# Gates as three rounded-fp32 products, two more pairs down in seven of eight products, and norm factors sent as rows through DRAM

## The chip, the core and the metric

The kernel runs on one core of a Trainium2 chip. The metric is the device time of one execution in microseconds; the time of the kernel before is the median of three runs. Five engines work side by side, each with its own queue in order: PE (matmuls), DVE, ACT and POOL (elementwise work), and SP, which here only issues DMAs. A DMA that waits for data holds back every later DMA of SP's queue.

## The reference

One step of a decoder layer for 2048 prompt tokens and 8 sampled tokens (together 2056), width D = 1024, all in fp32:

```python
xn = _rmsnorm(x, norm1_g)
z = einsum('btd,de->bte', xn, w_in)          # xr 512 | gr 512 | q 512 | k 128 | v 128
xr, gr, q, k, v = split(z, IN_SPLITS)
xc, new_conv = _causal_conv(xr, conv_buf, conv_w, conv_b)
...
r = sigmoid(_block_diag(xf, gate_a_w, gate_a_b))   # the two gates of the RG-LRU, 8 blocks of 64x64
i = sigmoid(_block_diag(xf, gate_x_w, gate_x_b))
... # h = a_t * h + u_t over the tokens
rec = hs * gelu(gr);  att = sliding-window attention(q, k, v)
mix = concatenate([_rmsnorm(rec, rec_norm_g), _rmsnorm(att, attn_norm_g)])
h = x + einsum('bte,ed->btd', mix, w_out)
hn = _rmsnorm(h, norm2_g)
ff = silu(hn @ w_gate) * (hn @ w_up)          # width 2816
y = h + ff @ w_down
...
y_prompt = _rmsnorm(yp, final_norm_g)
```

Every `_rmsnorm` needs one factor for each token, 1/sqrt(mean(x^2) + eps). The kernel keeps activations with features on the partitions and tokens along the columns, so a factor must be known on all 128 partitions, as one row repeated.

## The kernel before, in words

The work has two stages. **Stage A** (to about 610 us) goes through four token groups, `SUBS`, of 520, 512, 512 and 512 tokens. For each: normalise x, the input projection (`ip{s}_{u}`, u = 0 to 13: xr chunks are 0 to 3, gr chunks 4 to 7, then k, v and q), the recurrent part in four chunks of 128 channels (`rec_chunk`: convolution `xc`, the gates `g` on PE, tanh on ACT to `ra` and `ia`, the scan), attention, a norm of each part (`rc`, `at`), and the output projection `op`. **Stage B** is the FFN over three groups of two halves, 2 x 344, 2 x 342 and 2 x 342 tokens. Each group goes through 11 pairs of feature blocks; gate and up of a pair are made as seven products (`ps_g`, `ps_u`) instead of eight. The way down either takes 96 matmuls for a pair (`pd`), or, where `wino(gi, p)` holds, seven products instead of eight with 84 matmuls (`pw`), whose results are added into six buffers `y` by more additions on DVE. A final norm (`finish`, factors `f{group}_{half}`) ends each half; its result goes out as `out_yT`, and the next group's `y` starts from `hs` in DRAM.

A product that has to be as exact as fp32 is made of three products of rounded operands: with w = wh + wl and x = xh + xl, it is wh·xh + wl·xh + wh·xl (`mm3`, L990). Only the gates and the small matmuls of the norms are plain fp32, where one matmul instruction leaves two records in the trace.

A norm's factors are made with sums on PE (`st_`), a DVE addition and a POOL power (L1018, L1019), which leave them as a column for each block of tokens. `row_bcast` (L1021) then makes a plain fp32 matmul for each block: the column, broadcast, against an identity, which leaves the row on all partitions in PSUM (`bc_`); ACT copies it to `rb_` (L1033). `half_bcast` (L1042) does the same for the FFN's norm, cut to the halves (`hb`).

The order of the work is written out: the table `ORDER` lists for PE, DVE, ACT, POOL and SP what each issues in turn, and nothing is moved from that. PSUM has three accumulators (`acc`) for projections and single banks for the small things; `m` is the bank that gates, broadcasts and transposes share. All weight loads, the loads of `y`, and `out_yT` go through SP's queue.

Of the kernel before, what the change touches and what calls it, by code (L numbers as in the profile page):

```python
# [13 lines left out]
P = 128  # L14
# [23 lines left out]
TM = 520  # L38
# [15 lines left out]
U_R, R_AT = 0.875, 2  # L54
# [20 lines left out]
def wino(gi, p):  # L75
    return gi > 0 and 0 < p < NPAIR - 1


def plan():
    t, begin, end, prod, down, rounds = T_B0, [], [], {}, {}, {}  # L80
    for gi in range(len(HALVES)):
        begin.append(t)
        for p in range(NPAIR):
            mixed = p and wino(gi, p - 1)
            n = 0
            for i in range(14):
# [31 lines left out]
vt0_2 ip0_13_0:13 ip0_13_1:6 vt0_3 ip0_13_1:16 ip0_2_0 ip0_13_1 ip0_2_0 ip0_13_1 ip0_2_0:4 s0_0_0:2 ip0_2_0:2 s0_0_0
# [2141 lines left out]
```

## Time and profile before

| | |
|---|---|
| median of the runs | 2038.34 us (2037.39 to 2038.42) |
| profiled execution | 2035.2 us, its span 2033.4 us |
| mean granted clock of PE | 0.995 |
| busy PE, DVE, ACT, POOL | 2004.7, 1472.9, 955.0, 906.8 us |
| HBM | 221 GB/s over the span |

In lines of the trace an entry reads: engine, source line, operation, out<-in by the program's names, shape, count, then busy us and mean ns of one, then the idle time ahead and what ended it. In a timeline the first number is the start and the second the length. L963 is the helper that records every matmul, L968 that of transposes.

### The profile page before, as it was taken

The numbers are of one execution on the slowest core, as the hardware profiler recorded it, in microseconds if no ns is written. First come the engines' busy times: TensorE is split into PE (matmuls) and PEld (weight loads), VectorE is DVE, ScalarE is ACT, GpSimd is POOL, SyncE is SP. The second block draws the span as 40 slices with busy tenths as digits, with TensorE's granted clock in tenths as the row PEclk, the third lists the DMA queues.
The fourth block names the chain that finished last, engine by engine and source line by source line (L and its number), as shares of the span: only waits on it lengthen the run. The fifth ranks groups of instructions, "written<-read, shape, count | busy, mean of one in ns | idle before, by whom it ended". The sixth has DMA issues, their size and how long they took to land.

```text
span 2033.4 us, 34750 instructions
## 1 busy us (share of the span) xinstructions
PE 2004.7 (99%) x12273; PEld 1904.5 (94%) x12273; DVE 1472.9 (72%) x2694; ACT 955.0 (47%) x1960; POOL 906.8 (45%) x799
## 2 busy tenths in 40 slices
PE   9999999999999999999999999999999999999997
PEld 8988887888778999999999999999999999999997
DVE  6888986777886777765555777787767666776675
ACT  5776764654563543443344533343335433433443
POOL 4312451120132796676666645565557422322333
PEclk9999999999999999999999999999999999999999
DMA  9863675667688776764546687776668675555552
GB/s 338 297 215 127 225 273 182 210 197 223 206 288 272 285 245 208 240 212 168 184 172 224 229 282 242 261 240 214 228 209 290 204 236 196 182 197 199 195 173 101
DMA packets 208991, 450.98 MB, mean 222 GB/s; under 512 B 25232, under 2 KB 82720, under 8 KB 208800
## 3 DMA queue, kind: packets, MB, share of 16 engines
q1 hardware_dynamic: 205184, 445.73, 65.2%
q10 hardware_dynamic: 3632, 3.02, 0.5%
q8 instruction: 97, 1.59, 0.3%
q14 instruction: 78, 0.64, 0.1%
HBM read 335.89 MB, written 113.84 MB: 221 GB/s over the span
## 4 chain that ended last, share of the span: by engine, by line
PE 88%; DMA 6%; DVE 4%; issue 1%; ACT 1%; SPq 0%; DVEq 0%; ACTq 0%
PE ps_g L963 20%; PE ps_u L963 20%; PE ip L963 14%; PE pw L963 12%; PE pd L963 11%; PE op L963 5%; PE s L963 1%; DMA m<-mixed 1%; PE g L963 1%; PE pt L968 1%; PE o L963 1%; DMA mixed<-n 1%; DMA y<-hs 1%; DMA xs<-in_xT 0%; DMA hn<-mixed 0%
## 5 line engine op out<-in xcount | busy, mean ns | idle before, releaser
L963 PE MATMUL ps_g<-hn,w_g 128*128 128x342 f32 (+1 forms) x2772 | 546.0, 320 | 1.8 <-DMA w_g<-split_g 1.0
L963 PE MATMUL ps_u<-hn,w_u 128*128 128x342 f32 (+1 forms) x2772 | 529.8, 320 | 4.5 <-ACT c_u L1985 3.5
L963 PEld LDWEIGHTS ps_u<-hn,w_u 128*128 128x128 f32 x2772 | 455.0, 189 | 5.5 <-ACT c_u L1985 3.8
L963 PEld LDWEIGHTS ps_g<-hn,w_g 128*128 128x128 f32 x2772 | 456.6, 189 | 2.5 <-ACT w_d L1778 2.3
L963 PE MATMUL ip<-xn,w_in 128*128 128x512 f32 (+1 forms) x1680 | 367.3, 361 | 3.9 <-ACT w_in L936 2.7
L963 PEld LDWEIGHTS ip<-xn,w_in 128*128 128x128 f32 x1680 | 271.5, 190 | 49.4 <-issue 4.8
L2050 DVE TENSOR_TENSOR y<-y,pw 128x342 f32<-128x342 f32 x504 | 242.7, 506 | 94.8 <-PE pw L963 90.4
L963 PE MATMUL pd<-fh,w_d 128*128 128x344 f32 (+1 forms) x960 | 235.0, 320 | 0.0
L963 PE MATMUL op<-mix,w_out 128*128 128x512 f32 (+1 forms) x960 | 209.8, 362 | 0.3 <-DVE mix L999 0.3
L2021 DVE TENSOR_TENSOR y<-y,pd 128x344 f32<-128x344 f32 (+1 forms) x240 | 119.6, 509 | 103.3 <-PE pd L963 91.1
L963 PEld LDWEIGHTS op<-mix,w_out 128*128 128x128 f32 x960 | 157.6, 190 | 30.0 <-issue 6.1
L963 PE MATMUL pw<-fh,wd 128*128 128x342 f32 x576 | 167.5, 319 | 1.0 <-DVE y L2021 1.0
L963 PEld LDWEIGHTS pd<-fh,w_d 128*128 128x128 f32 x960 | 167.3, 188 | 0.0
L963 PE MATMUL pw<-t,wd 128*128 128x342 f32 x648 | 150.6, 319 | 0.0
L963 PE MATMUL pd<-fl,w_d 128*128 128x344 f32 (+1 forms) x480 | 147.6, 320 | 0.0
L1946 POOL TENSOR_TENSOR c_u<-c_u,c_g 128x342 f32<-128x342 f32 (+1 forms) x60 | 58.8, 980 | 180.2 <-DVE c_u L1964 144.5
L1964 DVE TENSOR_TENSOR c_u<-c_u,ps_u 128x342 f32<-128x342 f32 (+1 forms) x99 | 50.5, 510 | 122.1 <-PE ps_u L963 121.8
L1935 DVE TENSOR_TENSOR fl<-c_u,fh 128x342 fp32r<-128x342 f32 (+1 forms) x132 | 118.5, 909 | 15.3 <-ACT fh L1934 14.2
L1779 POOL TENSOR_TENSOR w_u<-ru,w_u 128x512 fp32r<-128x512 f32 x44 | 58.9, 1340 | 151.8 <-ACT w_u L1778 123.0
L1934 ACT CAST fh<-c_u 128x342 fp32r<-128x342 f32 (+1 forms) x132 | 62.1, 479 | 106.4 <-POOL c_u L1946 41.9
L963 PEld LDWEIGHTS pw<-t,wd 128*128 128x128 f32 x648 | 111.4, 189 | 0.0
L963 PEld LDWEIGHTS pw<-fh,wd 128*128 128x128 f32 x576 | 105.6, 189 | 1.3 <-DVE y L2021 1.3
(299 smaller groups left out, 3499.9 us busy)
## 6 DMA issues: line engine op xcount, KB each, us to landing
w_g<-split_g SPq DMA_DIRECT2D x88, 512.0 KB, 4.4
w_u<-split_u SPq DMA_DIRECT2D x88, 512.0 KB, 5.5
w_in<-split_w SPq DMA_DIRECT2D x84, 512.0 KB, 3.6
rg<-in_wgate SPq DMA_DIRECT2D x110, 256.0 KB, 3.1
ru<-in_wup SPq DMA_DIRECT2D x110, 256.0 KB, 3.3
w_out<-split_w SPq DMA_DIRECT2D x48, 512.0 KB, 4.8
split_g<-w_g SPq DMA_DIRECT2D x44, 512.0 KB, 2.8
split_u<-w_u SPq DMA_DIRECT2D x44, 512.0 KB, 2.9
```

Of the source, the lines that this page charges most:

```text
L963: r = nc.tensor.matmul(*args, **kw)
L968: r = nc.tensor.transpose(*args)
L1779: lo_eng.tensor_tensor(w[:, 1, :], src, w[:, 0, :].bitcast(F32), op=ALU.subtract)
L1934: nc.scalar.copy(hi, v)
L1935: nc.vector.tensor_tensor(lo, v, hi.bitcast(F32), ALU.subtract)
L1946: (nc.vector if p == NPAIR - 1 or src is not v else eng(E_MUL[2 * h + n])).tensor_tensor(v, src, g, op=ALU.mult)
L1964: nc.vector.tensor_tensor(o, a, b, op)
L2021: nc.vector.tensor_tensor(ys[gi, n, m], ys[gi, n, m], ps, ALU.add)
L2050: nc.vector.tensor_tensor(v, v, ps, ALU.add)
```

## The change

Three things, and a new order of everything.

1. The gates' weights `gw` are split once, in the prologue, into `gwh` (ACT) and `gwl` (POOL); for each chunk `xc` is split into `xch` (ACT copy, rounded) and `xcl` (POOL subtraction). Each of the 40 gate matmuls (24 of 512 columns, 16 of 260) becomes three of rounded operands.
2. `wino` now holds for the first pair of groups 1 and 2 too. Those two pairs go down with 84 matmuls each in place of 96. `R_FIRST` sets from which product of the next pair on their rounds are planned.
3. The factors of x1, x2, x3, rc1, rc2, f0, f1 and all of h go another way: PE transposes the columns to rows (`tr_`), ACT copies them to `row_`, SP writes them to DRAM (`rows_`), and SP reads them back, repeated on all partitions (`rb_`, `hb`). 12 bc_x, 8 bc_rc, 14 bc_f and 22 hb matmuls go; 13 transposes, 13 ACT copies, 13 writes and 15 reads come in, and 15 ACT copies of the broadcasts go.

```diff
-U_R, R_AT = 0.875, 2
+U_R, R_AT, R_FIRST = 0.875, 2, 6
...
 def wino(gi, p):
-    return gi > 0 and 0 < p < NPAIR - 1
+    return gi > 0 and p < NPAIR - 1
...
-                if mixed and i >= R_AT:
+                if mixed and i >= (R_AT if p > 1 else R_FIRST):
...
+        rowp = E(tc.tile_pool(name="rowp", bufs=2))
...
+        rows_h = dp.tile([1, NTOK], F32, name="rows_h")
+
+        def rows_out(row, cols, w, nt, name):
+            ps = m_tile(f"tr_{name}")
+            tr(f"tr_{name}", ps[:nt, :w], cols, ident[:w, :w])
+            v = rowp.tile([8, P], F32, tag="row", name=f"row_{name}")[:nt, :w]
+            nc.scalar.copy(v, ps[:nt, :w])
+            nc.sync.dma_start(row.rearrange("o (j p) -> (o j) p", p=w), v)
+
+        def dram_bcast(cols, w, nt, name):
+            row = dp.tile([1, w * nt], F32, name=f"rows_{name}")
+            rows_out(row, cols, w, nt, name)
+            out = bcp.tile([P, TM], F32, tag="bc", name=f"rb_{name}")
+            nc.sync.dma_start(out[:, :w * nt], row.to_broadcast([P, w * nt]))
+            return out
+
+        def h_rows(s):
+            c0, T, _, w, nt = SUBS[s]
+            rows_out(rows_h[:, c0:c0 + T], rs2[:w, s, :nt], w, nt, f"h{s}")
...
         def half_bcast(gi, n, name):
             o, nn = HALVES[gi][n]
             out = hbp.tile([P, TP], F32, tag="hb", name=f"hb_{name}")
-            ps = m_tile(f"hb_{name}")
...
-            nc.scalar.copy(out[:, :nn], ps[:, :nn])
+            nc.sync.dma_start(out[:, :nn], rows_h[:, o:o + nn].to_broadcast([P, nn]))
             return out
...
-            gw = ap1.tile([P, 1024], F32, name="gw")
+            gwh = ap1.tile([P, 1024], F32R, name="gwh")
+            gwl = ap1.tile([P, 1024], F32R, name="gwl")
...
-                nc.sync.dma_start(gw, gatew)
+                raw = bigp.tile([P, 2 * TM], F32, tag="big", name="graw")[:, :1024]
+                nc.sync.dma_start(raw, gatew)
+                nc.scalar.copy(gwh, raw)
+                nc.gpsimd.tensor_tensor(gwl, raw, gwh.bitcast(F32), op=ALU.subtract)
...
-                state[s]["bc"] = row_bcast(cols[:w, :nt], w, nt, f"x{s}")
+                state[s]["bc"] = (dram_bcast if s else row_bcast)(cols[:w, :nt], w, nt, f"x{s}")
...
+                xh = ap1.tile([P, TM], F32R, tag="xch", name=f"xch{s}_{c}")
+                xl = ap1.tile([P, TM], F32R, tag="xcl", name=f"xcl{s}_{c}")
+                nc.scalar.copy(xh[:, :T], xc[:, :T])
+                nc.gpsimd.tensor_tensor(xl[:, :T], xc[:, :T], xh[:, :T].bitcast(F32), op=ALU.subtract)
...
+                        wcols = slice((gi * 4 + c) * P, (gi * 4 + c + 1) * P)
...
-                            mm(f"g{s}_{c}_{gi}_{n0}", ps[:, :nn], gw[:, (gi * 4 + c) * P:(gi * 4 + c + 1) * P], xc[:, n0:n0 + nn],
-                                             start=True, stop=True)
+                            for i, (w, x) in enumerate(((gwh, xh), (gwl, xh), (gwh, xl))):
+                                mm(f"g{s}_{c}_{gi}_{n0}", ps[:, :nn], w[:, wcols], x[:, n0:n0 + nn], start=i == 0, stop=i == 2)
...
-                bc = row_bcast(cols[:w, :nt], w, nt, f"{name}{s}")
+                bc = (dram_bcast if name == "rc" and s in (1, 2) else row_bcast)(cols[:w, :nt], w, nt, f"{name}{s}")
...
                     rstd_cols(acc[:, :T], w, nt, 0, rs2[:w, s, :nt], f"h{s}")
+                    h_rows(s)
...
-                bc = row_bcast(cols[:w, :nt], w, nt, name, 0)
+                bc = dram_bcast(cols[:w, :nt], w, nt, name)
```

All rows of `ORDER` are new as well. Three places of it follow; each row is a source line, an operation and out<-in, and the brackets name what it waits for. The first is PE around the gates of token group 2, chunk 0, before:

```order
L963 MATMUL g2_0_0_0_3874<-xc2_0_3809,gw_132 128x512 [waits Activation_49]
L963 MATMUL ip2_1_0_3837<-xn2_3_3581,w_in2_1_0_3775 128x512
```

and now:

```order
L1044 MATMUL g2_0_0_0_3974<-xch2_0_3970,gwh_136 128x512 [waits Activation_49]
L1044 MATMUL g2_0_0_0_3974<-xch2_0_3970,gwl_137 128x512
L1044 MATMUL ip2_1_0_3933<-xn2_4_3675,w_in2_1_1_3873 128x512 [waits DMAHW1_49]
L1044 MATMUL ip2_1_0_3933<-xn2_4_3675,w_in2_1_1_3873 128x512
L1044 MATMUL g2_0_0_0_3974<-xcl2_0_3971,gwh_136 128x512 [waits Pool_49]
```

One matmul became three, and the third, which needs POOL's subtraction, stands two projection products behind the second.

The second place is DVE in the same stretch, where token group 1's recurrent part (`rrec`) is multiplied by its norm factors `rb_rc1`, and the accumulators of group 2's projections are emptied (`xr2_1` is the one of ip2_1, the `rrec` rows with ip2_4 and ip2_5 those of these two). Before:

```order
L1418 SCALAR_TENSOR_TENSOR rrec_144<-rrec_144,vec_99,rb_rc1_3766 128x512 [waits Activation_49]
L1418 SCALAR_TENSOR_TENSOR rrec_144<-rrec_144,vec_99,rb_rc1_3766 128x512
L1421 TENSOR_TENSOR mix1_0_3780<-rrec_144,mix1_0_3780 128x512 [waits Activation_49]
L1537 TENSOR_TENSOR ptl7_1_1_2651<-pt7_1_1_2645,pth7_1_1_2650 128x512 [waits Activation_49]
L1315 TENSOR_TENSOR rrec_144<-ip2_4_0_3692,rb_x2_3607 128x512 [waits DVE_49]
```

and now:

```order
L1635 TENSOR_TENSOR ptl7_1_1_2708<-pt7_1_1_2702,pth7_1_1_2707 128x512 [waits Activation_49]
L1516 SCALAR_TENSOR_TENSOR rrec_149<-rrec_149,vec_102,rb_rc1_3867 128x512 [waits DMAHW5_49]
L1408 TENSOR_TENSOR xr2_1_3869<-ip2_1_0_3933,rb_x2_3702 128x512 [waits PE_49]
L1519 TENSOR_TENSOR mix1_0_3876<-rrec_149,mix1_0_3876 128x512 [waits Activation_49]
L1408 TENSOR_TENSOR rrec_149<-ip2_4_0_3787,rb_x2_3702 128x512 [waits DVE_49]
```

The wait for ACT's copy became a wait for a DMA, and the accumulator of ip2_1 is emptied right behind it rather than several steps later. On PE, `tr_rc1` stands where `bc_rc1` stood, and ip2_8 is the first that waits for `xr2_1`.

The third place is SP's queue at the start of FFN group 1, where the final norm of group 0 (`f0`) meets the loads of group 1. Before, with the loads of `y1_0` some 40 rows further ahead:

```order
L2071 DMA out_yT<-y0_1_8121 128x344 [waits DVE_49]
L2071 DMA out_yT<-y0_5_8205 128x344 [waits DMAHW3_49,DVE_49]
L1802 DMA w_u1_1_6_13367<-split_u_115 128x1024 [waits DMAHW4_49,PE_49]
```

and now, up to the first of the `y1_0` loads:

```order
L2170 DMA out_yT<-y0_5_8358 128x344 [waits DMAHW4_49,DVE_49]
L1124 DMA rows_f0_0_13364<-row_f0_0_13367 4x86 [waits DMAHW5_49,Activation_49]
L1901 DMA w_u1_1_5_13500<-split_u_118 128x1024 [waits DMAHW6_49]
L1996 DMA sums_d_119<-sd0_1_13358 128x512 [waits DMAHW7_49]
L1958 DMA rd1_1_7_13598<-in_wdown 128x256 [waits DMAHW0_49,DVE_49]
L1130 DMA rb_f0_0_13370<-rows_f0_0_13364 128x344 [waits DMAHW5_49,DMAHW1_49]
L1873 DMA y1_0_13303<-hs_115 128x342 [waits DMAHW4_49,DMAHW2_49]
```

The read of the row waits on SP until the row's write has landed, and the loads of `y1_0` come behind it. On DVE the first addition into `y1_0` follows the first use of `rb_f0_0`.

More of the change, by code (lines that the diff above doesn't have):

```diff
@@ new lines @@
+w1_0_5_1 g1_1_3:2 w1_0_5_0 g1_1_3:7 u1_1_1 g1_1_3:2 u1_1_1:9 g1_1_4 u1_1_1 g1_1_4:9 tr_f0_0 g1_1_4:2 u1_1_6:10 u1_1_2
+u1_1_6:2 u1_1_2:3 w1_0_2_0 u1_1_2:6 w1_0_2_0:2 u1_1_2:2 u1_1_5:12 u1_1_7:12 w1_0_6_0:3 w1_0_1_3:3 w1_0_6_1:3 u1_1_4:2
+w1_0_7_0:3 u1_1_4:10 u1_1_3:7 g1_2_1:2 u1_1_3:5 g1_2_1:10 g1_2_2:12 w1_0_6_3:3 w1_0_7_1:3 w1_0_3_0:3 w1_0_4_0:3
+w1_0_3_1:3 w1_0_2_1:2 w1_0_7_3:3 w1_0_1_2:3 w1_0_2_1 w1_0_4_1:3 w1_0_5_2:2 w1_0_6_2:3 w1_0_2_2:2 w1_0_5_2 w1_0_2_2
+w1_0_7_2:3 w1_0_5_3:3 w1_0_3_2:3 g1_2_5:11 w1_0_3_3:3 w1_0_4_2:3 w1_1_5_0 g1_2_6:2 w1_0_2_3:3 w1_1_1_0:3 g1_2_6
@@ L746 @@
+wd2.8:2 wu2.8 wg2.9+4 wu2.9 wg2.9 wd2.8 wg2.9 wd2.8 wg2.9 wu2.9 wg2.9 wd2.8 wg2.10 wu2.9+4 wg2.10 wd2.9:3 wu2.9
+wd2.9:2 wu2.9:3 wg2.10+4 wu2.10 wg2.10 wd2.9+1 wg2.10 wd2.9 wg2.10 wu2.10 wg2.10 wd2.9 wd2.10 wu2.10+4 wd2.10:3
+wu2.10:4 f21:8 f20:4
 """,
```

1350 lines of the change are left out of this document (706 added, 644 removed).

## The prediction

> **What bounds the kernel now.** I read the page's busy table and its chain first, then stretches of the span.
>
> ```profile
> PE 2004.7 (99%) x12273; PEld 1904.5 (94%) x12273; DVE 1472.9 (72%) x2694; ACT 955.0 (47%) x1960; POOL 906.8 (45%) x799
> ...
> PE 88%; DMA 6%; DVE 4%; issue 1%; ACT 1%; SPq 0%; DVEq 0%; ACTq 0%
> ```
>
> PE is busy for 99% of the span and is 88% of the chain that ended last. So the time is PE's work plus the few places where PE waits; other engines matter only through those places. The next view gives busy time by stretch (sum, instructions; then granted clock, DMA share, GB/s).
>
> ```profile
> 200.00:250.00 50.00, 49.82 (x328) 44.20 (x327) 47.88 (x76) 38.49 (x70) 20.49 (x17) 1.00 0.65 214
> 600.00:700.00 100.00, 93.48 (x478) 81.62 (x479) 69.00 (x106) 47.26 (x96) 44.54 (x32) 0.95 0.85 294
> 1100.00:1200.00 100.00, 97.37 (x633) 96.56 (x632) 69.57 (x106) 44.99 (x100) 59.34 (x53) 1.00 0.79 267
> ```
>
> PE waits mostly around 600 to 700 us (6.5 us) and at the start of the second group (2.6 us). From 200 to 250 us DVE is nearly as full as PE, which becomes a rival below. The waits themselves, and the clock behind the two largest:
>
> ```profile
> 596.67 0.66 PE L968 MATMUL pt<-cs,sc 128*128 128x128 f32 x4 [2.11 <-DVE ptl L1537]
> 680.45 1.25 PE L963 MATMUL ps_u<-hn,w_u 128*128 128x344 f32 x4 [3.55 <-ACT c_u L1985]
> 1183.28 0.71 PE L963 MATMUL ps_u<-hn,w_u 128*128 128x342 f32 x3 [0.82 <-DMA w_u<-split_u]
> 1199.19 0.42 PE L963 MATMUL pw<-fh,wd 128*128 128x342 f32 x1 [1.04 <-DVE y L2021]
> 681.00:685.00 4.00, 4.00 (x18) 4.00 (x17) 0.94 (x2) 1.96 (x5) 2.49 (x3) 0.60 1.03 405
> 610.00:614.00 4.00, 3.67 (x11) 2.93 (x12) 3.42 (x8) 3.44 (x7) 1.52 (x1) 0.50 0.34 76
> ```
>
> Behind the 3.55 us wait the granted clock is 0.60 for 4 us, which costs another 1.6 us; behind the waits near 600 it is 0.50 for 4 us, another 2 us. Waits near 1 us leave no such mark (1100 to 1200 has 1.00). The Trainium skill, "TensorE: Matmul & The Clock Gate", section "What's actually happening", says that an idle window of about 3.4 us halves the clock until a busy window has passed; the two rows agree, and no run here shows more.
>
> **Paces.** Matmul records overlap, so a group's busy sum is too large. I use the time from end to end in dense stretches.
>
> ```profile
> 391.80 8.12 PE op L963 x35
> ...
> 1572.70 8.91 PE pd L963 x57
> ```
>
> A 512-column product of rounded operands takes 8.12/35 = 0.232 us, a 342-column one 8.91/57 = 0.156 us. Plain fp32 is next; it makes two records for each matmul.
>
> ```profile
> 43.31 0.60 PE L963 MATMUL g<-xc,gw 128*128 128x260 f32 x2
> 43.56 2.88 PE L963 MATMUL ip<-xn,w_in 128*128 128x260 f32 x21
> 46.27 0.60 PE L963 MATMUL g<-xc,gw 128*128 128x260 f32 x2
> 317.71 8.05 PE L963 MATMUL ip<-xn,w_in 128*128 128x512 f32 x34
> 325.60 1.02 PE L963 MATMUL g<-xc,gw 128*128 128x512 f32 x2
> 278.73 0.38 PE L963 MATMUL bc_x<-cs,xcols 128*128 128x128 f32 x2
> 278.95 0.27 PE L968 MATMUL pt<-cs,sc 128*128 128x128 f32 x1
> 279.06 0.83 PE L963 MATMUL bc_x<-cs,xcols 128*128 128x128 f32 x6
> ```
>
> The 21 260-column products end at 46.44, the gate before them at 43.91: 0.120 us each. The gate behind them ends at 46.87: 0.43 us for one. For 512 columns: 325.76 to 326.62, 0.86 us. The last six broadcast records end at 279.89, the transpose before them at 279.22: 0.67/3 = 0.22 us for a plain 128x128 matmul. The transpose ends 0.11 us after the two records before it (279.11): 0.11 us for one.
>
> **The change part by part: PE's work.** The counts of what goes are records, two for one matmul:
>
> ```profile
> L963 PE MATMUL g<-xc,gw 128*128 128x512 f32 x48 | 24.6, 594 | 0.2 <-ACT ra L1354 0.2
> L963 PE MATMUL g<-xc,gw 128*128 128x260 f32 x32 | 9.6, 382 | 0.0
> L963 PE MATMUL bc_x<-cs,xcols 128*128 128x128 f32 x24 | 4.1, 273 | 0.0
> L963 PE MATMUL bc_rc<-cs,rccols 128*128 128x128 f32 x24 | 3.5, 274 | 0.0
> L963 PE MATMUL bc_f<-cs,cols_f 114*128 114x114 f32 x24 | 3.8, 275 | 1.8 <-DVE cols_f L2103 1.8
> L963 PE MATMUL bc_f<-cs,cols_f 86*128 86x86 f32 x16 | 2.2, 268 | 0.0
> L963 PE MATMUL hb<-cs,rs 128*128 128x128 f32 x16 | 2.9, 283 | 0.0
> ```
>
> Gates: 24 of 512 columns become three products, 0.86 - 3 x 0.232 = 0.16 us less each, 3.9 us; 16 of 260 columns, 0.43 - 0.36 = 0.07, 1.1 us. Together **-5.0**.
> Down: in groups 1 and 2 the first pair's 96 products become 84, 24 fewer at 0.156: **-3.8**.
> Broadcasts: 12 of bc_x, 8 of the 12 of bc_rc, 14 of the 20 of bc_f and all 22 of hb go (12 of these have at least 104 columns, ten are pieces of 2 to 126). Full ones at 0.22 are 12 + 8 + 12 = 32, 7.0 us. The narrower 14 and 10 lie between 0.15 and 0.22; at 0.19, 4.6 us. 13 transposes come in at 0.11, 1.4 us. Together **-10.2** (bounds -9.2 to -11).
> Sum **-19.0 us of PE work**, some 11 before 650 us and 8 in the FFN. PE has no other cover: what leaves it shortens the end unless a new wait takes it.
>
> **Work added on the other engines.** 16 ACT casts and 16 POOL subtractions for the low parts, of the kind of the next row, about 20 us on POOL over 600 us where it works less than half the time (20.49 of 50 above).
>
> ```profile
> L1779 POOL TENSOR_TENSOR w_u<-ru,w_u 128x512 fp32r<-128x512 f32 x44 | 58.9, 1340 | 151.8 <-ACT w_u L1778 123.0
> ```
>
> The subtraction takes 1.34 us, but only the third product needs it, and that stands 0.2 to 2 us of PE work behind the second; the gates of a chunk are spread among input projections. I price this at 0, up to 0.3 us for each of eight chunks if POOL is late (2.4 us). The first chunk's gates are the worst: POOL and ACT also split the gate weights and the w_in blocks there, and the head already waits. Up to 2 us more, or none. DVE gets 24 more additions to y, but the seven products spread them; 0.
>
> **The rows through DRAM.** Before, PE makes the broadcast and ACT copies it. Now a factor goes transpose, ACT copy, write on SP's queue, read on SP's queue. No row of this size exists; the nearest are small writes, and reads of 171 KB from DRAM (us to landing last). The copy is bounded by its wider kin.
>
> ```profile
> out_sconv_o<-xr ACTq DMA_DIRECT2D x4, 4.0 KB, 4.7
> out_sh_o<-q ACTq DMA_DIRECT2D x4, 4.0 KB, 3.0
> n<-hs SPq DMA_DIRECT2D x32, 171.0 KB, 3.5
> y<-hs SPq DMA_DIRECT2D x32, 171.0 KB, 5.3
> 1168.08 0.45 ACT L1033 COPY rb_f<-bc_f 128x344 f32<-128x344 f32 x1 [1.30 <-PE bc_f L963]
> ```
>
> So a trip is 0.1 + 0.45 + (3.0 to 4.7) + (3.5 to 5.3) = 7.1 to 10.6 us, plus up to 1 us in ACT's queue. The Trainium skill, "DMA: Bandwidth & Descriptors", section "Anatomy of one DMA", gives about 2.0 us fixed for a DMA, most of it the write's receipt, so two would take 4 us, no trip would make PE wait, and the sum below would be 4 us lower, 2017. The rows above are 1 to 3 us slower than that for each transfer; by them the trace disagrees, and I go by the rows.
>
> Most trips have room: x2, x3, rc2 and all of h are used tens of us later. Four do not.
> For rc1, DVE now waits for rb_rc1 (second excerpt of the change) ahead of the eviction of ip2_1, which the next projection waits for. Between the transpose and that projection stand 40 products, 40 x 0.232 = 9.3 us. Trip and two DVE steps of 0.7 make 8.5 to 13; PE waits 0 to 3.7. Before, the same two lay like this:
>
> ```profile
> 305.23 1.42 DVE L1418 SCALAR_TENSOR_TENSOR rrec<-rrec,vec,rb_rc 128x512 f32<-128x512 f32 x2 [0.68 <-ACT rb_rc L1033]
> 313.34 0.69 DVE L1315 TENSOR_TENSOR xr<-ip,rb_x 128x512 f32<-128x512 f32 x1 [2.05 <-PE ip L963]
> ```
>
> I take 1.5. For x1 the next eviction that needs it has 10.5 us of PE work ahead of it and no such queue: 0 to 1, 0.5. At the start of group 1, SP waits with rb_f0_0 for the written row, and behind it stand y1's loads, the out_yT writes and w_u1_1_3 (third excerpt); DVE's first addition into y1 waits for both. From tr_f0_0 to the product that needs this addition are 64 products, 10.0 us; trip, issue and two DVE steps make 9 to 13. PE waits 0 to 3; I take 1.2. Group 2 likewise, 0.8. Sum of new waits **+4** (0 to 12, with 2.4 for POOL's subtractions). Against them the old waits at the same places, 0.82 and 1.04 above and about as much at the third group, partly go, since the broadcasts that PE itself made and the late pd additions are gone: **-2** (0 to -3).
>
> Sum: 2035.2 of the profiled execution - 19.0 + 4 - 2 = 2018.2. The median of the runs is 3.1 above that execution (2038.34), so **2021 us**; with no new wait and 3 of the old ones gone 2016, with all bounds high and no old one gone 2031.
>
> **Rivals.**
> *The waits near 600 to 700 us shrink too.* The tables of all engines are new, and the two largest places cost 3.55 + 1.6 and, with the three waits behind 596, about 4.7 + 2, 11.9 in all with their clock. If half goes: 2021 - 6 = **2015**, at best 2009. For it: nothing but the fresh order; against it: DVE's ptl chain there is the same.
> *Trips at their long end.* All waits at their bounds, 12 instead of 4, of which two over 3 us drop the clock as at 681 (1.6 each): 2021 + 8 + 3.2 = **2032**.
> *DVE binds in 200 to 300 us.* At 47.88 of 50 it has 2 us to spare, and a PE that needs 3 us less there meets it; the stage's gain of 11 would shrink to about 5: **2027**. Against it: the other stretches of the stage have room.
> *Slower: SP's queue is held.* Each of 13 row writes stands in SP's queue ahead of weight loads until ACT has copied, and its read until the write has landed. If loads behind were just in time, as the one that cost 0.82, PE would lose the hold each time. The gain of 19 is gone at 19/13 = 1.5 us for each; at 3.0, the shortest landing, the time is 2021 + 39 = **2060**, at 1.7 **2043**. Against it: in the first stage loads are issued some 10 us ahead.
> *The gates' products are no cheaper* (the form runs at the plain pace): +5, **2026**. The op rows at 0.232 speak against it.
>
> **How the numbers follow.** Forecast 0.56; waits shrink 0.13; long trips 0.16; DVE or the gates' pace 0.07; SP held 0.08. The range 2010 to 2033 holds all but most of the last and the lower end of the second. A measurement of this kernel can tell about 0.2%, 4 us: faster takes the first four less 0.04, 0.88; same 0.05; slower 0.07.
>
> **What would show it.** PE's busy sum falls by about 19 to 20 us and its gates make 72 and 48 records. The reads rb_rc1, rb_f0 and rb_f1 land 7 to 11 us behind their transposes; the waits in front of ip2_8 and of the pw products at the start of groups 1 and 2 stay under 3 us, the clock near them 1.00. The forecast is wrong if PE's idle grows by over 10 us, if weight loads on SP become releasers in the first stage, or if PE's work falls by less than 15.

## The result, and the profile after

The changed kernel takes **2021.83 us** (median of four runs, 2019.98 to 2024.3) against 2038.12 for the kernel before in the same session (2037.39 to 2038.42): a ratio of 0.9921, 95% interval 0.9904 to 0.9939. The forecast was 2021, range 2010 to 2033. The profiled execution of the changed kernel took 2019.98 us, its span 2018.2, 15.2 less than before. The first thing is where these 15.2 us came from, because it was not quite from where the prediction had them.

The page of the changed kernel, busy table and chain:

```profile
PE 1990.2 (99%) x12190; PEld 1892.4 (94%) x12190; DVE 1477.3 (73%) x2733; ACT 963.7 (48%) x1987; POOL 946.8 (47%) x829
...
PE 88%; DMA 4%; DVE 4%; issue 1%; ACT 1%; POOL 1%; SPq 0%; DVEq 0%; ACTq 0%; POOLq 0%
```

PE is still 99% busy and 88% of the chain. Its busy sum fell by 14.5 us and its idle by 0.7 (28.7 to 28.0). The busy sum is a poor scale here: a record that runs at half clock counts as busy, and so does the 0.26 us by which a matmul behind a gap fails to overlap the one before it (the lone `pw` record of 0.42 us in the rows of "SP's loads first", against a pace of 0.16). So I use one more quantity. For each PE record, take the time from the end of the record before to its own end, and subtract the pace for its columns (0.232 us for 512, 0.157 for 342, 0.120 for 260, about 0.11 for 128, 0.43 for a record of a plain fp32 gate). The sum is the **loss**: gaps, refills and slow clock together. The span less the loss is the **work**. Here they are for every profiled execution of this study, in us; the losses are split by place (0 to 100 is the head, 500 to 700 the junction of the two stages, 1100 to 1200 and 1600 to 1700 the starts of groups 1 and 2):

| kernel | span | work | loss | head | 300-400 | 400-500 | 500-700 | 1100-1200 | 1600-1700 |
|---|---|---|---|---|---|---|---|---|---|
| before | 2033.4 | 2000.3 | 33.1 | 8.0 | 0.1 | 0.2 | 15.0 | 3.1 | 0.1 |
| changed | 2018.2 | 1980.5 | 37.7 | 9.0 | 1.3 | 0.2 | 9.9 | 7.1 | 4.3 |
| changed, once more | 2022.1 | 1980.3 | 41.8 | 10.2 | 1.7 | 0.2 | 9.8 | 10.7 | 3.2 |
| f on PE | 2017.2 | 1983.1 | 34.1 | 9.3 | 1.3 | 0.2 | 10.9 | 4.5 | 2.2 |
| SP's loads first | 2025.9 | 1980.3 | 45.6 | 9.9 | 1.2 | 0.2 | 10.4 | 12.9 | 5.8 |
| gates in fp32 | 2025.5 | 1985.7 | 39.8 | 9.7 | 1.7 | 0.3 | 8.7 | 9.1 | 3.7 |
| x and rc on PE | 2019.2 | 1984.3 | 34.9 | 10.4 | 0.1 | 0.2 | 8.3 | 7.5 | 3.1 |
| f and rc1 on PE | 2017.0 | 1984.1 | 32.9 | 10.4 | 0.1 | 0.2 | 8.6 | 6.2 | 2.1 |
| one hop more for rc1 | 2020.1 | 1980.3 | 39.8 | 9.8 | 4.6 | 0.2 | 11.4 | 4.9 | 3.1 |
| one hop more for x2, x3, rc2, h | 2026.1 | 1980.6 | 45.5 | 9.1 | 2.4 | 2.9 | 10.6 | 11.0 | 3.3 |
| one hop more for f | 2031.4 | 1980.6 | 50.8 | 9.8 | 1.4 | 0.2 | 11.1 | 12.1 | 10.5 |

Read it from the work column first. Kernels with the same PE work agree within 0.3 us (1980.3 to 1980.6, five of them), so the split into work and loss is sharp. It rests on the paces named: other paces for the small records shift all rows together, by up to some 3 us, and the differences between rows by some tenths, so only the differences count. The change took **19.8 us of work** out and **added 4.6 us of loss**, which is the 15.2. The losses moved in both directions: the junction lost 5.1 less, the two group starts 8.2 more.

Four of these stretches in the view by windows of the changed kernel (PE's busy time and instructions first; granted clock, DMA share and GB/s last):

```profile
500.00:600.00 100.00, 96.49 (x479) 78.50 (x478) 89.67 (x192) 62.83 (x127) 24.30 (x30) 0.99 0.80 254
600.00:700.00 100.00, 99.72 (x521) 89.21 (x520) 65.41 (x100) 47.66 (x97) 54.00 (x39) 0.96 0.87 305
1100.00:1200.00 100.00, 95.47 (x600) 92.45 (x599) 77.41 (x134) 41.34 (x93) 65.32 (x61) 1.00 0.84 276
1600.00:1700.00 100.00, 97.85 (x612) 95.46 (x612) 73.45 (x148) 34.70 (x71) 28.43 (x24) 1.00 0.76 247
```

From 600 to 700 PE's idle went from 6.5 us to 0.3; from 1100 to 1200 from 2.6 to 4.5; and 1600 to 1700, full before, has 2.2. The waits behind these, from PE's timeline:

```profile
311.18 2.12 PE L1044 MATMUL ip<-xn,w_in 128*128 128x512 f32 x8 [1.01 <-DVE xr L1408]
...
599.41 1.11 PE L1049 MATMUL pt<-cs,sc 128*128 128x128 f32 x4 [1.89 <-DVE ptl L1635]
...
1163.47 4.01 PE L1044 MATMUL ps_u<-hn,w_u 128*128 128x342 f32 x24 [1.34 <-DMA w_u<-split_u]
...
1170.45 0.74 PE L1044 MATMUL pw<-t,wd 128*128 128x342 f32 x3 [1.68 <-DVE y L2149]
...
1178.48 2.56 PE L1044 MATMUL ps_g<-hn,w_g 128*128 128x342 f32 x12 [0.78 <-ACT w_g L1877]
...
1611.10 2.30 PE L1044 MATMUL ps_u<-hn,w_u 128*128 128x342 f32 x13 [1.10 <-DMA w_u<-split_u]
```

The wait of 3.55 us at 680 in the kernel before, and the slow clock behind it, are gone. In their place stand smaller ones at the group starts, named after loads, after DVE's additions to `y` and after ACT. Two of the new trips, from the timeline of all engines; rc1's and f0_0's, the later of the two at the start of group 1:

```profile
300.53 0.27 PE L1049 MATMUL tr_rc<-cs,rccols 128*4 128x128 f32 x1
301.12 0.27 SPq L1124 DMA_DIRECT2D rows_rc<-row_rc  x1
305.03 0.32 SPq L1130 DMA_DIRECT2D rb_rc<-rows_rc  x1
309.78 0.75 DVE L1516 SCALAR_TENSOR_TENSOR rrec<-rrec,vec,rb_rc 128x512 f32<-128x512 f32 x1 [5.72 <-DMA rb_rc<-rows_rc]
...
1156.92 0.24 PE L1049 MATMUL tr_f<-cs,cols_f 86*4 86x86 f32 x1
1157.57 0.27 SPq L1124 DMA_DIRECT2D rows_f<-row_f  x1
1161.03 0.32 SPq L1130 DMA_DIRECT2D rb_f<-rows_f  x1
1166.08 0.58 DVE L2169 SCALAR_TENSOR_TENSOR y<-y,vec,rb_f 128x344 f32<-128x344 f32 x1 [3.33 <-DMA rb_f<-rows_f]
```

Both take 9.2 us from the start of the transpose to the first use: 0.6 to the issue of the write, 3.9 and 3.5 until the read can be issued, 4.8 and 5.1 until DVE starts. In both, DVE stood and waited for the read.

### The profile page after: what moved, and what is told of

It is laid out like the page before. It is cut to its first block, busy times and chain, and to the rows that moved or that the text cites. A ratio compares the mean times of both kernels' runs of the same rounds, so it can differ in the third digit from the quotient of the medians.

```text
span 2018.2 us, 34697 instructions
## 1 busy us (share of the span) xinstructions
PE 1990.2 (99%) x12190; PEld 1892.4 (94%) x12190; DVE 1477.3 (73%) x2733; ACT 963.7 (48%) x1987; POOL 946.8 (47%) x829
## 4 chain that ended last, share of the span: by engine, by line
PE 88%; DMA 4%; DVE 4%; issue 1%; ACT 1%; POOL 1%; SPq 0%; DVEq 0%; ACTq 0%; POOLq 0%
PE ps_g L1044 21%; PE ps_u L1044 20%; PE ip L1044 12%; PE pw L1044 12%; PE pd L1044 10%; PE op L1044 8%; PE s L1044 1%; PE o L1044 1%; PE pt L1049 1%; PE g L1044 1%; DMA y<-hs 1%; DMA m<-mixed 0%; DMA mixed<-n 0%; DMA rg<-in_wgate 0%; POOL w_in L1018 0%
## 5 line engine op out<-in xcount | busy, mean ns | idle before, releaser
L1044 PE MATMUL ps_g<-hn,w_g 128*128 128x342 f32 (+1 forms) x2772 | 570.2, 320 | 1.8 <-ACT w_g L1877 1.3
L2149 DVE TENSOR_TENSOR y<-y,pw 128x342 f32<-128x342 f32 x560 | 267.2, 505 | 103.9 <-PE pw L1044 96.7
L1044 PE MATMUL pd<-fh,w_d 128*128 128x344 f32 (+1 forms) x832 | 200.8, 320 | 0.0
L1044 PE MATMUL pw<-fh,wd 128*128 128x342 f32 x640 | 188.3, 320 | 0.1
L1044 PE MATMUL pw<-t,wd 128*128 128x342 f32 x720 | 180.8, 320 | 1.8 <-DVE y L2149 1.7
L2120 DVE TENSOR_TENSOR y<-y,pd 128x344 f32<-128x344 f32 (+1 forms) x208 | 102.7, 509 | 79.8 <-PE pd L1044 78.4
L1044 PEld LDWEIGHTS pd<-fh,w_d 128*128 128x128 f32 x832 | 144.3, 188 | 0.2
L1044 PEld LDWEIGHTS pw<-t,wd 128*128 128x128 f32 x720 | 126.1, 189 | 2.9 <-DVE y L2149 2.6
L1044 PE MATMUL pd<-fl,w_d 128*128 128x344 f32 (+1 forms) x416 | 123.3, 320 | 0.0
L1946 ACT CAST wd<-rd 128x512 fp32r<-128x512 f32 x110 | 68.2, 620 | 90.3 <-PE ps_u L1044 35.8
```

Source lines behind the costliest of these rows:

```text
L1044: r = nc.tensor.matmul(*args, **kw)
L1946: nc.scalar.copy(w[:, :, 0], v)
L2120: nc.vector.tensor_tensor(ys[gi, n, m], ys[gi, n, m], ps, ALU.add)
L2149: nc.vector.tensor_tensor(v, v, ps, ALU.add)
```

## The experiments

What was open: whether the new waits come from the row trips or from the new order of SP's queue, whether each term of the work was priced rightly, whether DVE had come to bind, and how near the far trips are to costing something. Everything below is an edit of the changed kernel; where an instruction is replaced, its replacement stands at its place in the written order.

### The final norm's factors back on PE

```diff
 def finish(...):
-                bc = dram_bcast(cols[:w, :nt], w, nt, name)
+                bc = row_bcast(cols[:w, :nt], w, nt, name, 0)
```

> The changed kernel, but the four norm factors f0 and f1 go as before: 14 plain matmuls and an ACT copy of the broadcast in place of transposes and the trip through DRAM. PE's work rises by 14 x 0.2 - 4 x 0.11 = 2.3 us. Theory A (the trip sets the waits at the start of groups 1 and 2): these waits, 7.1 us over pace in 1100 to 1200 and 4.3 in 1600 to 1700, fall back to about the 3.1 and 1.4 of the kernel before; net -4 to -5 us against the changed kernel's 2021.8, about 2017. Theory B (the first pair going down in seven products needs y earlier and fills the queues, whatever brings the factors): the waits stay, net +2, about 2024. Theory C (weight loads queued behind rows on SP): the waits for w_u near 1163 and 1611 go (2.9), those for y stay, net -1.

Measured: 2018.76 us (2017.33 to 2023.26), ratio 0.9917, 0.9904 to 0.9931. The work rose by 2.6. The loss at the two group starts is 6.7 us against 11.4 in the changed kernel's profile. PE's waits there:

```profile
1169.77 0.74 PE L1044 MATMUL pw<-t,wd 128*128 128x342 f32 x3 [0.67 <-DVE y L2149]
1173.36 1.37 PE L1044 MATMUL ps_u<-hn,w_u 128*128 128x342 f32 x7 [0.44 <-DMA w_u<-split_u]
1178.16 2.56 PE L1044 MATMUL ps_g<-hn,w_g 128*128 128x342 f32 x12 [0.75 <-ACT w_g L1877]
```

The wait for `y` fell from 1.68 to 0.67 us and the one for `w_u` from 1.34 to 0.44, while the last, for ACT's `w_g`, did not move (0.78, 0.75): it has nothing to do with the trip. So by this profile the trip holds part of this loss but not all of it: with f on PE 6.7 us are left, 3.5 more than before the change. Neither expected time came. By the ratios (0.9917 against 0.9921) the time moved by less than 1 us, where theory A had 4 to 5 less and B 2 more; the two intervals overlap, so the trip saves about as much work as it costs in waits.

### SP's loads first

In SP's written order, three loads of `w_u` are moved ahead of `out_yT` writes and rows at the starts of groups 1 and 2 (shown as names in SP's order):

```diff
+ w_u_1_7<-split_u
+ w_u_1_5<-split_u
  out_yT<-y_3
- w_u_1_7<-split_u
  out_yT<-y_5
  rows_f_0<-row_f_0
- w_u_1_5<-split_u
...
  rows_f_0<-row_f_0
+ w_u_1_5<-split_u
  out_yT<-y_5
  out_yT<-y_0
  out_yT<-y_3
- w_u_1_5<-split_u
```

> The changed kernel, with three weight loads moved forward in SP's queue: w_u1_1_7 and w_u1_1_5 ahead of the out_yT write that waits for DVE, w_u2_1_5 ahead of three out_yT writes. Nothing else moves. Theory C (loads queued behind rows on SP): PE's waits for w_u at 1163.5 (1.57 over pace) and 1611.1 (1.37) go and stay gone: -2.5 to -3 us, about 2019. Theory A (the row trip and the y chain behind it end last): the waits for w_u go but PE waits as long for DVE's addition into y a few us later: within 1 us of the changed kernel, 2021 to 2022.

Measured: 2026.13 us (2023.5 to 2027.66), ratio 0.9948, 0.9935 to 0.996. It is slower than the changed kernel, by an amount just clear of the noise, which neither theory had said. The waits for `w_u` at 1163 and 1611 did go. But PE then met the wait for `y`, three times within five microseconds and for as long in sum as theory A had it, and the granted clock fell. PE's timeline, with an earlier wait first, and the windows behind each:

```profile
1148.39 0.42 PE L1044 MATMUL pw<-fl,wd 128*128 128x342 f32 x1 [1.76 <-DVE fl L2034]
...
1171.41 0.73 PE L1044 MATMUL pw<-t,wd 128*128 128x342 f32 x3 [1.53 <-DVE y L2149]
1172.91 0.42 PE L1044 MATMUL pw<-fh,wd 128*128 128x342 f32 x1 [0.76 <-DVE y L2149]
1174.54 1.22 PE L1044 MATMUL pw<-t,wd 128*128 128x342 f32 x3 [0.90 <-DVE y L2149]
```

```profile
1150.00:1154.00 4.00, 4.00 (x19) 3.84 (x18) 2.99 (x6) 0.60 (x2) 1.51 (x2) 0.58 0.05 18
1174.00:1178.00 4.00, 3.46 (x12) 3.46 (x13) 3.25 (x7) 0.00 (x0) 0.92 (x1) 0.50 0.93 326
1178.00:1182.00 4.00, 4.00 (x20) 4.00 (x19) 1.93 (x3) 0.62 (x1) 1.18 (x1) 0.67 0.96 296
```

In the changed kernel the three waits of 1.34, 1.68 and 0.78 us end 7 and 8 us apart, and the clock stays at full speed between them:

```profile
1166.00:1170.00 4.00, 2.68 (x16) 2.12 (x14) 3.92 (x7) 2.19 (x5) 1.73 (x2) 1.00 1.01 308
1170.00:1174.00 4.00, 3.55 (x22) 3.46 (x23) 3.52 (x7) 0.31 (x1) 1.67 (x2) 1.00 0.93 328
```

Waits of about the same sum were dearer where they lay close together. The 3.2 us of waits for `y` here were followed by some 8 us at 0.50 and 0.67, about 3.3 us more (4 x 0.5 + 4 x 0.33). The Trainium skill, "TensorE: Matmul & The Clock Gate", section "What's actually happening", describes the clock as set by how busy PE was in a free-running window of about 3.4 us. That three waits of 0.76 to 1.53 us within 4.7 us were followed by half clock, without one gap of that length, agrees with a window that counts activity; the table of that section speaks of an idle window, which these rows do not bear out.

Not all of this profile's loss comes from the edit. Of the 5.8 us more from 1100 to 1200, some 3 lie ahead of the first load that was moved, which SP issues at 1159.79: PE waited 1.76 us for DVE's `fl`, 0.33 in the changed kernel, and the clock behind it was 0.58. DVE came late there by a wait for a transfer (1.29 us against 0.90) and an operation of 1.62 us in place of 0.53, neither of which the edit touches. Whether the other four runs have this wait is not known, so how much of the median's 5 us the moved loads cost stays open.

### The gates in plain fp32

```diff
-                nc.scalar.copy(xh[:, :T], xc[:, :T])
-                nc.gpsimd.tensor_tensor(xl[:, :T], xc[:, :T], xh[:, :T].bitcast(F32), op=ALU.subtract)
...
-                            for i, (w, x) in enumerate(((gwh, xh), (gwl, xh), (gwh, xl))):
-                                mm(f"g{s}_{c}_{gi}_{n0}", ps[:, :nn], w[:, wcols], x[:, n0:n0 + nn], start=i == 0, stop=i == 2)
+                            mm(f"g{s}_{c}_{gi}_{n0}", ps[:, :nn], gwh[:, wcols], xc[:, n0:n0 + nn], start=True, stop=True)
```

> The changed kernel, but each of the 40 gate matmuls is one plain fp32 matmul again at the place of the first of its three; the copies and subtractions that split xc are left out. If the term was right, PE's work rises by 24 x 0.16 + 16 x 0.07 = 5.0 us and the time with it, to about 2027. Rival: the three products are no cheaper, or PE was waiting for the subtractions: 2022 or less. If POOL's and ACT's splitting caused part of the waits in the head and near 311 us, these shrink and the rise is only 3 to 4.

Measured: 2027.77 us (2027.32 to 2030.82), ratio 0.9962, 0.995 to 0.9975. The work rose by 5.2 us; the prediction had 5.0. This count uses the prediction's own pace for a plain gate, but with a wrong one the loss where gates stand would have changed, and the head, 300 to 400 and 400 to 500 have 9.7, 1.7 and 0.3 against 10.2, 1.7 and 0.2 in the changed kernel's repeat. By the ratios the time rose by 7 to 9 us. Of the rest, 1.3 us are new loss from 100 to 300 (2.7 where the other kernels have some 1.5): PE waits 0.91 us for DVE's addition into `xres` at 270, which it does not in the changed kernel. The losses at the group starts, 12.8 against 11.4 and 13.9 in the changed kernel's two profiles, vary from run to run.

### x and rc back on PE

```diff
-                state[s]["bc"] = (dram_bcast if s else row_bcast)(cols[:w, :nt], w, nt, f"x{s}")
+                state[s]["bc"] = row_bcast(cols[:w, :nt], w, nt, f"x{s}")
...
-                bc = (dram_bcast if name == "rc" and s in (1, 2) else row_bcast)(cols[:w, :nt], w, nt, f"{name}{s}")
+                bc = row_bcast(cols[:w, :nt], w, nt, f"{name}{s}")
```

> The changed kernel, but x1 to x3, rc1 and rc2 go as before: 20 plain 128x128 matmuls in place of 5 transposes and trips. PE's work rises by 20 x 0.22 - 5 x 0.11 = 3.9 us. Theory of the prediction: the wait of 1.0 us ahead of ip2_8 (311.2 us) goes, the rest lies on the path: net +2.9, about 2024.7. Rival (DVE binds from 200 to 300 us, so PE's work there counts for nothing): 2021 to 2022.

Measured: 2023.04 us (2020.53 to 2025.65), ratio 0.9935, 0.9922 to 0.9949. The work rose by 3.8. The loss from 300 to 400 us went from 1.3 back to 0.1, as before the change, so the wait at 311 is the rc1 trip and nothing else. From 200 to 300 us PE is busy for 99.7 of 100 us here and in the changed kernel alike, so DVE leaves PE room there and the rival of a binding DVE falls. The time rose by 2 to 3 us by the ratios, near the 2.9 expected, but the intervals overlap.

### The changed kernel once more

> The changed kernel itself, as the yardstick of this group of runs on the same chip: 2020 to 2023, with the waits of 7 us at 1100 to 1200 and 4 us at 1600 to 1700 once more.

Measured: 2023.37 us (2020.19 to 2023.88), ratio 0.9925, 0.9909 to 0.9941, in agreement with the first. Its profiled execution is 3.9 us longer, and the table says where: the start of group 1, 10.7 instead of 7.1. The same program, at the same place, has its waits for `y` split differently, and closer together:

```profile
1168.82 0.74 PE L1044 MATMUL pw<-t,wd 128*128 128x342 f32 x3 [0.94 <-DVE y L2149]
1170.79 0.42 PE L1044 MATMUL pw<-fh,wd 128*128 128x342 f32 x1 [1.22 <-DVE y L2149]
1172.42 1.22 PE L1044 MATMUL pw<-t,wd 128*128 128x342 f32 x3 [0.67 <-DVE y L2149]
```

```profile
1170.00:1174.00 4.00, 2.54 (x8) 2.11 (x9) 4.00 (x8) 0.00 (x0) 2.00 (x2) 0.64 0.90 300
1174.00:1178.00 4.00, 4.00 (x16) 4.00 (x16) 1.18 (x4) 0.00 (x0) 0.00 (x0) 0.51 0.87 253
```

So this kernel's time varies from run to run at a place where the spacing of a few waits goes with whether the clock drops. It also sets a bound on what one profile can show: the loss at this place has to differ by more than about 4 us before one profile tells it.

### f and rc1 back on PE, the rest as changed

```diff
-                bc = (dram_bcast if name == "rc" and s in (1, 2) else row_bcast)(cols[:w, :nt], w, nt, f"{name}{s}")
+                bc = (dram_bcast if name == "rc" and s == 2 else row_bcast)(cols[:w, :nt], w, nt, f"{name}{s}")
...
-                bc = dram_bcast(cols[:w, :nt], w, nt, name)
+                bc = row_bcast(cols[:w, :nt], w, nt, name, 0)
```

> The changed kernel with f0, f1 and rc1 made on PE as before: the five factors whose trip has no room. PE's work rises by 2.5 us for f and 0.45 for rc1; the waits of 4.7 us at the group starts and of 1.2 us ahead of ip2_8 go. If both waits come from the trip, net -3 us against the changed kernel of the same group; if the gain of the f variant was chance, 0 to +1.

Measured: 2020.37 us (2017.38 to 2022.71), ratio 0.9916, 0.9898 to 0.9934, against 0.9925 for the changed kernel on the same chip. It pays 3.8 us more work than the changed kernel's second profile and loses 8.9 less, of which 1.6 from 300 to 400 and 5.6 at the group starts. The median is 3 us lower and the ratio the lowest of the study, a hair under that of f on PE alone (0.9917); it beats the kernel before, but the interval overlaps the changed kernel's, so that it beats that one too is likely and not shown.

### One hop more for rc1

The written row is copied to a second row in DRAM before it is read.

```diff
+HOPS = ('rc1',)
...
-            rows_out(row, cols, w, nt, name)
+            if name in HOPS:
+                row0 = dp.tile([1, w * nt], F32, name=f"rows0_{name}")
+                rows_out(row0, cols, w, nt, name)
+                nc.sync.dma_start(row, row0)
+            else:
+                rows_out(row, cols, w, nt, name)
```

> The changed kernel with one more hop through DRAM for rc1 alone: the row is copied in DRAM before it is read. If the trip's length sets the wait ahead of ip2_8 (theory of the prediction), that wait of 1.2 us grows by the whole hop, 3 to 4 us, to 4 to 5, and the time by as much, more if the granted clock drops behind it. If the wait has another cause (DVE's queue), it stays near 1.2.

Measured: 2025.04 us (2021.96 to 2027.66), ratio 0.9937, 0.9917 to 0.9957. SP's, DVE's and PE's rows:

```profile
306.41 0.52 SPq L1132 DMA_DIRECT2D rows_rc<-rows_rc  x1
308.25 0.33 SPq L1136 DMA_DIRECT2D rb_rc<-rows_rc  x1
312.38 0.75 DVE L1522 SCALAR_TENSOR_TENSOR rrec<-rrec,vec,rb_rc 128x512 f32<-128x512 f32 x1 [7.50 <-DMA rb_rc<-rows_rc]
...
313.79 2.45 PE L1045 MATMUL ip<-xn,w_in 128*128 128x512 f32 x5 [2.79 <-DVE xr L1414]
```

The hop itself took 1.8 us, and PE's wait rose from 1.01 us to 2.79, by all of it. With the trip on PE the loss from 300 to 400 is 0.1, with one hop through DRAM 1.2 to 1.7, with two 4.6: a dose and its answer. The loss grew by about 3 us, more than the hop, since the clock behind the wait was 0.73 and 0.84 from 312 to 320. The trip of rc1 has no room left at all, and every tenth that it takes longer is PE's. The time rose by some 2 us by the ratios, with intervals that overlap: the trace shows the effect, the time alone does not. The expectation had the mechanism and took the hop for 3 to 4 us.

### One hop more for the far trips

The same extra hop for x2, x3, rc2 and all four rows of h (`HOPS = ('x2', 'x3', 'rc2')`, and `rows_h0` copied to `rows_h`).

> The changed kernel with one more hop through DRAM for seven factors: x2, x3, rc2 and the four rows of h. SP's queue waits for each hop too, some 3 us seven times. The prediction says that these trips have room: within 1 us of the changed kernel. The rival of the held queue (each hold of SP makes later weight loads late) says up to 7 x 3 = 21 us more.

Measured: 2027.87 us (2023.42 to 2029.82), ratio 0.9951, 0.9933 to 0.9968. The median is 4.5 us above the changed kernel's of the same session, neither within 1 us nor near 21; the intervals just overlap. Its profile stands 4.0 us above, of which 2.7 lie in 400 to 500, a place where neither kernel of that session had a loss. The rows there, of SP, DVE, POOL and PE:

```profile
439.40 0.27 SPq L1126 DMA_DIRECT2D rows_rc<-row_rc  x1
442.21 0.49 SPq L1133 DMA_DIRECT2D rows_rc<-rows_rc  x1
445.66 0.33 SPq L1137 DMA_DIRECT2D rb_rc<-rows_rc  x1
449.90 0.75 DVE L1524 SCALAR_TENSOR_TENSOR rrec<-rrec,vec,rb_rc 128x512 f32<-128x512 f32 x1 [3.71 <-DMA rb_rc<-rows_rc]
451.43 0.15 DVE L1100 TENSOR_SCALAR rs<-st_h 128x4 f32<-128x4 f32 x1
451.66 1.74 POOL L1101 TENSOR_TENSOR rs<-rs,nhalf 128x4 f32<-128x4 f32 x1 [7.73 <-DVE rs L1100]
453.46 0.27 PE L1050 MATMUL tr_h<-cs,rs 128*4 128x128 f32 x1 [1.98 <-POOL rs L1101]
```

Here is a chain that the prediction did not have. DVE waits for rc2's rows; three instructions behind that wait stands the addition for h's factor; POOL waits for it with its power; and PE waits for POOL with the transpose of h. The stalled engine is PE, the instruction named is one of another norm, and the cause is rc2's trip, held back some 3 us by the hop. In the changed kernel's repeat the same DVE instruction already waits:

```profile
446.56 0.75 DVE L1516 SCALAR_TENSOR_TENSOR rrec<-rrec,vec,rb_rc 128x512 f32<-128x512 f32 x1 [0.72 <-DMA rb_rc<-rows_rc]
```

So rc2, which the prediction counted among the far trips, is not far: it had no slack on DVE, and PE, which lost 2.1 us of the hop's 3, was within about 1 us of waiting. Another 0.7 us lie in 300 to 400, at rc1, whose own path has no extra hop here. SP's rows:

```profile
299.84 0.85 SPq L1143 DMA_DIRECT2D rows_h<-rows_h  x1
302.53 0.33 SPq L1154 DMA_DIRECT2D hb<-rows_h  x1
...
303.80 0.28 SPq L1126 DMA_DIRECT2D rows_rc<-row_rc  x1
```

SP stood at h's read until h's extra copy had landed, and rc1's write, whose transpose began at 301.08, was issued only at 303.80, 2.7 us behind it instead of 0.6. This is the held queue of the slower rival, for less than 1 us of PE. It is there once more: the remaining 0.6 us of the 2.7 is a wait of rc2's own transpose (0.40 us at 438.81). Ahead of it DVE stood 0.82 us at the first use of x3's row, until a transfer had landed that SP issued behind x3's hop, which had held SP from 423.4 to 428.0. The other hops show no new loss that this profile could tell; 500 to 700, where most of h is used, does not move beyond what other runs have (10.6 against 9.8).

### One hop more for f

`HOPS = ('f0_0', 'f0_1', 'f1_0', 'f1_1')`, otherwise as above.

> The factors f0 and f1 (the starts of groups 1 and 2) make one hop more through DRAM: the written row is copied to a second DRAM row before it is read, four hops in all; everything else as in the changed kernel. In the run with the extra hop for rc1 a hop took about 1.9 us and PE's wait grew by all of it. Theory A (the trips set PE's waits at the group starts): both trips of a group stand in the same queue, so y is later by 2 to 4 us at each group; PE's waits at 1100 to 1200 and 1600 to 1700 grow by 4 to 8 us together, more if they bunch and the granted clock drops, as where SP's loads were put first; the time is 4 to 9 us over the changed kernel, 2026 to 2031. Rival B (the loads of w_u behind the reads set them, and the trip for y has room): the loads that stand behind the reads come later by the hop too, so the waits named after w_u grow and those named after y do not; the time is 2024 to 2027. Rival C (the group-start waits come from DVE's queue and not from the trip): no difference beyond 1 us, 2021 to 2024.

Measured: 2032.18 us (2027.56 to 2036.94, ten runs), ratio 0.9979, 0.9968 to 0.9991. Nearly the whole gain of the change is gone, and the loss at the group starts is 22.6 us, against 11.4 and 13.9. Rival C is out, and B's limit of 2027. What B named does happen, the waits for `w_u` grew from 2.4 us to 5.0 in sum, but the waits that come over DVE grew more, as A had it; A's upper end of 2031 is passed by the median all the same. DVE's and PE's rows, and the windows at the start of group 2:

```profile
1170.89 0.58 DVE L2175 SCALAR_TENSOR_TENSOR y<-y,vec,rb_f 128x344 f32<-128x344 f32 x1 [5.68 <-DMA rb_f<-rows_f]
1175.86 0.74 PE L1045 MATMUL pw<-t,wd 128*128 128x342 f32 x3 [2.27 <-DVE y L2155]
...
1623.86 2.03 DVE L2175 SCALAR_TENSOR_TENSOR y<-y,vec,rb_f 128x342 f32<-128x342 f32 x4 [6.06 <-DMA rb_f<-rows_f]
1625.81 0.69 DVE L1884 TENSOR_TENSOR w_g<-rg,w_g 128x512 fp32r<-128x512 f32 x1
1626.55 3.22 PE L1045 MATMUL ps_g<-hn,w_g 128*128 128x342 f32 x10 [4.00 <-DVE w_g L1884]
```

```profile
1622.00:1626.00 4.00, 0.55 (x2) 0.27 (x2) 2.14 (x5) 0.26 (x1) 0.00 (x0) 0.79 0.98 306
1626.00:1630.00 4.00, 3.45 (x12) 3.45 (x13) 4.00 (x9) 0.19 (x1) 0.92 (x1) 0.50 1.03 306
```

The longest wait of the run, 4.00 us, is put down to `w_g`, the low part of a gate weight, which has nothing to do with f. But that subtraction stands behind four products with `rb_f` in DVE's queue, and DVE waited 6.06 us for `rb_f`. This is how the trip reaches PE at a group start: not only by the `y` that is late, but by whatever else DVE holds behind it. Then the clock is at 0.50 for 4 us, another 2 us.

## Why the prediction was right, and where it was not

**The time** came out as forecast (2021.83 against 2021). Two terms that were left out or set too low cancelled, so the sum was better than its parts.

**PE's work, -19.0: right.** The work fell by 19.8 us. The gates by themselves 5.2 (5.0 had been said), x and rc 3.8 (12 and 8 broadcasts less 5 transposes at the prices given are 3.9), f 2.6. What is left, 8.2, belongs to the first pairs and to h together, for which the prediction had 3.8 and some 4. These two were not undone one by one. The counts support the pairs: down matmuls of 342 columns, `pd` and `pw`, fell by 24. That the gates' products would be no cheaper is refuted.

**What lay on other engines at no price: right.** The gates show no wait in the profile's groups, neither for ACT's casts nor for POOL's subtractions; the head's loss grew by 1.0 us in the first profile and 2.2 in the second, about the 2 that were given at most. With the gates in plain fp32 it is 9.7 all the same, so the splitting of `xc` is not what grew it; what did is not known.

**The trip, 7.1 to 10.6 us: right but for one.** 9.2 us at rc1 and at f0_0, 7.1 and 10.0 at f1_1 and f1_0, 8.1 at rc2 (438.48 to 446.56 in the repeat), but 5.7 at f0_1. The shorter sum from the fixed cost on the Trainium skill's "DMA: Bandwidth & Descriptors", section "Anatomy of one DMA", would have had no wait for rc1; the 1.0 us wait, which vanishes when rc1 is made by PE, says otherwise. That section gives its figure for DMAs that GpSimd issues, which the prediction did not say; these are issued by SP. At rc1 and f0_0 the write alone held the read back by 3.9 and 3.5 us, at f0_1 by at most 1.3.

**rc1, 1.5: right** (1.3 to 1.7 us with its refill), and shown by taking the trip away and by lengthening it. **x1, 0.5:** none seen.

**"x2, x3, rc2 and all of h are used tens of us later": wrong for rc2.** DVE waits for it already; PE was 1 to 2 us from waiting. I had looked at the consumer of the row and not at what stands behind that consumer in DVE's queue.

**The group starts, +1.2 and +0.8 with -2 for the old waits: the mis-sized term.** The sum of these was 0 and measured +6.9 (1100 to 1200 +4.0, 1600 to 1700 +4.2, 1500 to 1600, where an old wait went, -1.3) in the first profile and +9.4 in the second. The mechanism given was one of several. The trip does set part of it: with f on PE the loss there is 6.7 and 8.3 in two kernels, with the trip between 8.0 and 14.3 in six profiles (18.7 with SP's loads first), with an extra hop 22.6. The first two ranges touch, so it is the extra hop that shows it. The step failed in two ways. I priced one waiting product for each group, where DVE's queue passes the delay to several (additions to `y`, low parts of weights), and I did not see that such waits, each near 1 us, cost clock as soon as they lie close together. The sentence "waits near 1 us leave no such mark" holds for single ones only, and the kernel before had the counterexample: the 0.50 from 610 to 614 stands behind waits of 0.50, 0.92 and 1.19 us that end at 605.85, 607.27 and 610.33. So that row did not agree with an idle window of 3.4 us, as the prediction says; only the row behind the 3.55 us wait did. About 3.5 to 5 us of the loss, by the two kernels with f on PE, do not come from the trip; the wait for ACT's `w_g` is one of them. Whether they belong to the first pairs' additions or to the new order was not told apart.

**The rival "waits near 600 to 700 shrink": it happened,** with 5.1 us where half had been put at 6. It was given 0.13. In the kernel before, the largest of them hung on a transfer, as ACT's timeline of that kernel shows just ahead of PE's wait (the row names a load; a write of `hs` had landed 0.2 us earlier):

```profile
679.96 0.45 ACT L1985 COPY c_u<-ps_u 128x344 f32<-128x344 f32 x1 [4.18 <-DMA m<-mixed]
```

A wait that hangs on transfers in a stretch where the DMA engines are crowded (share 0.85) may go with any new order of the queues, while the ones behind ptl, which hang on DVE's own chain, did survive (1.89 at 599, with the clock at 0.50 behind). I had argued from the second to both. The 3.55 us wait is absent from all ten profiles with the change, whether or not gates, x, rc or f are undone, so none of these alone removed it; the rows of h and the new order remain as candidates, and were not separated.

**The rival of SP's held queue: seen twice, small.** Seven extra hops cost 4 us of span together and not one hop's length each, and of that 2.1 by DVE's queue and some 1.3 by SP's. At the group starts, where the loads of `w_u` stand behind rows and reads, moving the loads forward moved the wait and did not save it.

**The signs.** The gates' 72 and 48 records, the arrival 7 to 11 us behind the transposes of rc1, f0_0 and both f1, and waits under 3 us with clock 1.00 came true in the first profile; f0_1 was in use after 5.7 us, and in the second profile the clock near the waits was 0.51. That PE's busy sum would fall by 19 to 20 us did not (14.5): slow and refilled records count as busy, and the sign should have been the work and not the busy sum.

## What to carry to other kernels

Before a value is sent through memory instead of over an engine, follow the in-order queue of the engine that will wait for it: what stands behind the waiting instruction is delayed with it, and PE's stall then bears the name of something else. A trip with no slack puts all that it lasts longer on PE, and one with slack costs nothing, so a broadcast that saves PE a microsecond or less should go through DRAM only where its first use, and the next use of everything queued behind it, is well over 10 us away. Where the sum is right, check its terms all the same: here a left-out gain of 5 us stood against an under-priced loss of 7.

## What the runs showed of the hardware that was not expected

Waits of about 1 us left the granted clock alone one at a time and not in a bunch: three that end 7 to 8 us apart (1.34, 1.68, 0.78 us) left it at 1.00; three within 5 us (0.94, 1.22, 0.67 in one execution, 1.53, 0.76, 0.90 in another kernel) were followed by some 8 us at 0.50 to 0.67. Where the border lies is open: three shorter ones within 5 us (1.10, 0.56 and 0.28 at the start of group 2 in the changed kernel) left it at 1.00, and a single wait of 1.76 us (SP's loads first) was followed by 4 us at 0.58, one of 1.89 us (at 599 in the changed kernel) by 8 us at 0.50.

A copy of 1 to 2 KB from DRAM to DRAM took between 1.8 us (rc1) and 4.6 us (x3) from its issue to the issue of the read behind it. A row's write from SBUF held its read back by at most 1.3 us (f0_1) and up to 4.5 us (x1) in the changed kernel. The trip of f0_1 took 5.7 us in all where rc1's and f0_0's took 9.2: its write held the read back by 2.2 to 2.7 us less, and the rest was about 1 us shorter. Why is open.
